# Two-layer hybrid trunk: rope tables kept on chip, deeper staging, inverses stored from two queues, waits of the side chains set anew

## The chip, the core and the metric

The kernel runs on one core of one Trainium2 chip. The metric is the device time of one execution in microseconds (us). TensorE is called PE, VectorE DVE, ScalarE ACT, GpSimd POOL, SyncE SP. SP issues nearly all DMAs; ACT issues a few. Each engine takes its instructions in the order of its own list, so an instruction that waits holds up all that stand behind it.

## The reference, cut to what matters

The model is two layers over 1024 tokens of width 1024 and 256 context tokens. Each layer projects the input by one wide matrix, runs three branches, merges them and normalizes.

```python
def _layer(...):                                  # twice
    u = x * (1 + scale) + shift                   # from silu(c) @ w_ada
    P, Pc = split_cols(u @ w_in), split_cols(uc @ w_in)
    q, k = axial_rope(P['a_q']), axial_rope(P['a_k'])
    y_a = band_ctx_attention(q, k, v, kc, vc, sink) * silu(P['a_z'])     # 8 heads, band of 128 and context
    y_b = layer_norm(depthwise_conv31(a * sigmoid(b))) ... * silu(P['b_z'])
    for d in range(2):                            # gated delta rule forwards and backwards
        T = triangular_solve(eye + A, eye)        # unit lower triangular, per chunk and head
        u, w = T @ (v * beta), T @ (k * beta * exp(gc))
        # scan over chunks: v_new = u - w @ S;  o = q_dec @ S + aqk @ v_new;  S = S * c_dec + k_dec^T @ v_new
    y_c = rmsnorm(o_forward + o_backward) * silu(P['c_z'])
    out = sum(sigmoid(gate_r) * (y_r @ w_branch[r]) for r in range(3)) @ w_out
    x = layer_norm(ALPHA * x + gate * out) * ln_g + ln_b
```

All arithmetic is float32. Dense products are made on PE as three products of a high and a low part (hi*hi, lo*hi, hi*lo).

## The kernel before

Channels lie on partitions, tokens on the free axis, in chunks of 256 (context), 512 and 512 tokens. A layer is a queue of dense pieces and a number of side chains, and PE's list is written by a planner while the program is built. The dense pieces (`main`) are projections of 128 output channels each: gates, gains, `aq`, `glu`, then the merge with `w_branch` and `finish` with `w_out`. The side chains are the recurrent delta branch (`delta1`, the inversion `invert`, `d2prep`, two `d2scan`), the attention units, the conformer and the norms. Each chain is a generator. After a step it yields a number of nanoseconds, and the planner puts at least that much estimated PE work, from `main` or from other chains, between this step and the chain's next one. These numbers stand in the table `W`, one for each layer:

```python
        if self.active and (self.active[0][0] <= self.pe or blocked or not self.main):
            c = self.active[0]
            self.pe = max(self.pe, c[0])
            ...
                w = next(c[2])
                c[0] = self.pe + (w or 0.0)
```

So PE's list is fixed, and on the chip PE waits whenever what a step needs comes later than the work put ahead of it. The order on DVE, ACT and SP is set by a scheduler when the program is built.

The places that the change touches:

- `load_half` (L236) loads half of a weight piece (`wraw`), ACT rounds it to `whi` (L244), DVE makes `wlo` (L247). Four buffers each.
- `rope` (L525) turns q and k. It loads 512 columns of the cosine and sine tables each time into `rtab`, of which there is one buffer; `conformer` uses the same buffer for `xt`.
- The tag `th` has three buffers of 128x512. They hold what goes out to or comes in from DRAM: `gth`, `fth`, `bth`, `r0`, `vr`, `vs`, `ar`, and in the merge `gt`.
- `invert` (L779) inverts the 32x32 diagonal blocks of both directions in 31 steps on DVE (`iU`), copies their transpose on ACT (`iV`, L819), and stores both to `sUB` by eight DMAs, all issued by ACT (L823).
- `d2prep` (L843) loads ten chunks of these blocks (`uc`), spreads them over block-diagonal tiles on DVE (`ud`, `ut`, `uh`), and joins them to full inverses by four rounds of products, with copies to `z`, `ut` and `ud` on ACT and DVE between. Its waits are `prep0` to `prep5`. `d2scan` takes the inverses (`scan1` to `scan3`).
- `attention` (L1133) loads K and V of one of two groups of heads into staging tiles of the tag `ks` (two buffers), makes K1, K2 and VH of them, and spawns one `att_unit` per 128 queries, two at a time. A unit loads `qs` (tag `ks` again), makes Q, waits `atq`, does its score products (`sd<-K,Q`, `ats` between heads), the softmax on DVE and ACT, waits `atm`, and transposes the weights and multiplies by V (`atp` between key blocks).
- `merge` (L1317) loads the branch results `y`, splits them (`yh`, `yl`), and multiplies by `w_branch`; it allocates the sums `acc` first.

DMAs from whatever engine take one of eight semaphores in turn (DMAHW0 to DMAHW7), and a DMA is issued only when the one that used its semaphore before has landed.

Of the kernel before, what the change touches and what calls it, by code (L numbers as in the profile page):

```python
# [8 lines left out]
F32 = mybir.dt.float32  # L9
# [3 lines left out]
ALU = mybir.AluOpType  # L13
# [4 lines left out]
P = 128  # L18
# [69 lines left out]
def constants():  # L88
# [6 lines left out]
    for d in range(2):  # L95
# [16 lines left out]
W = dict(rstd1=(510.0, 340.0), rstd2=(2820.0, 8120.0), adac=(6000.0, 11180.0), ss0=(15520.0, 10070.0),  # L112
         ss1=(560.0, 840.0), d1e=(3500.0, 3500.0), d1l=(2500.0, 2500.0), d1m=(1290.0, 880.0), d1t=(1120.0, 1270.0),
         prep0=(3500.0, 3500.0), do1=(17680.0, 17680.0), do2=(17680.0, 22350.0), atq=(3100.0,
         3540.0), ats=(2220.0, 1150.0), atm=(13300.0, 19000.0), atp=(1480.0, 1130.0),
         cf1=(38080.0, 38080.0), cf2=(5090.0, 12740.0), ln0=(2450.0, 4070.0), ln1=(1220.0,
         2790.0), ln2=(1120.0, 6710.0), d1s=(9710.0, 2570.0), dos=(9100.0, 20460.0),
         cfs=(139420.0, 35240.0), d2s=(20000.0, 20000.0), ada0=(35880.0, 35080.0),
         ln3=(9880.0, 13400.0), prep1=(2400.0, 2400.0), prep2=(2400.0,
         2400.0), prep3=(2200.0, 2200.0), prep4=(4500.0, 4500.0), prep5=(4000.0, 4000.0), scan1=(1540.0, 1540.0),  # L120
         scan2=(3090.0, 2630.0), scan3=(1380.0, 2190.0), ng=(9, 7), ln4=(1060.0, 1390.0),
         ln5=(1580.0, 130.0), g0=(3, 3), g1=(6, 6), g2=(16, 12), dvt=(13, 16), half=(0, 1),
         flight=(2, 2),
         inv0=(8000.0, 8000.0), inv1=(4000.0, 4000.0), inv2=(2300.0, 2300.0))


class Trunk:
# [4 lines left out]
    def __init__(self, ctx, tc, I, out, dbg=None):  # L132
        self.ctx, self.tc, self.nc, self.I, self.out = ctx, tc, tc.nc, I, out
        self.dbg = dbg or {}
        nc = self.nc
        ent = ctx.enter_context
        self.cst = ent(tc.tile_pool(name="cst", bufs=1))
        self.res = ent(tc.tile_pool(name="res", bufs=1))
        self.wp = ent(tc.tile_pool(name="wp", bufs=2))
        self.tp = ent(tc.tile_pool(name="tp", bufs=2))  # L140
        self.pp = ent(tc.tile_pool(name="pp", bufs=1, space=PSUM))
        self.dr = ent(tc.tile_pool(name="dr", bufs=1, space=DRAM))
        c = self.cst.tile([P, C_N], F32, name="consts")
        nc.sync.dma_start(c[:, :C_BAND], I["consts"][:, :C_BAND])
        self.late = lambda: nc.sync.dma_start(c[:, C_BAND:], I["consts"][:, C_BAND:])
# [223 lines left out]
    def first(self, S):  # L369
# [15 lines left out]
        with self.phase("ada0") as ph:  # L385
# [21 lines left out]
            self.late()  # L407
# [18 lines left out]
    def kv(self, l, S, ready):  # L426
# [4 lines left out]
        def back(c0, n, r):  # L431
            ps = self.sdps()
            for i in range(n // P):
                self.tr(ps[:, i * P:(i + 1) * P], r[:, i * P:(i + 1) * P])
            s = self.tp.tile([P, 512], F32, tag="th", name="vs", bufs=3)
            nc.scalar.activation(s[:, :n], ps[:, :n], AF.Copy)
            nc.sync.dma_start(S["V"][:, c0 // P:(c0 + n) // P, :], s[:, :n].rearrange("p (t c) -> p t c", c=P))

        def put(which, ps, c0, n):
            if which == 0:  # L440
                self.rope(ps, c0, n, lambda r, c0, n: nc.sync.dma_start(S["K"][:, c0:c0 + n], r))
                return
            r = self.tp.tile([P, 512], F32, tag="th", name="vr", bufs=3)
            nc.scalar.activation(r[:, :n], ps[:, :n], AF.Copy)
            pend.append((c0, n, r))
# [54 lines left out]
        for grp in ((CH_C, CH_A), (CH_B,)):  # L500
# [12 lines left out]
            for c0, n in grp:  # L513
# [8 lines left out]
                r = self.tp.tile([P, 512], F32, tag="th", name="ar", bufs=3)[:32]  # L522
# [258 lines left out]
    def invert(self, l, S, ph):  # L781
# [27 lines left out]
        for j in range(31):  # L809
# [283 lines left out]
    def glu(self, l, S, i, bg):  # L1093
# [15 lines left out]
    def gain(self, l, S, r, i):  # L1109
# [3 lines left out]
        def sink(ps, c0, n):  # L1113
            th = self.tp.tile([P, 512], F32, tag="th", name="fth", bufs=3)
# [17 lines left out]
    def attention(self, l, S, ph):  # L1132
# [8 lines left out]
        for g in range(2):  # L1141
            K1 = ph.tile([P, T], F32R, tag="K1", name="K1")
            K2 = ph.tile([P, T], F32R, tag="K2", name="K2")
            for c0, n in FULL:
                ks = ph.tile([P, 640], F32, tag="ks", name="ks", bufs=2)
# [5 lines left out]
            vs = ph.tile([P, NT, 64], F32, tag="ks", name="vs", bufs=2)  # L1151
# [4 lines left out]
            for t in range(0 if l < DEPTH - 1 else 2, NT):  # L1156
# [3 lines left out]
                self.spawn(name, self.att_unit(ph, S, g, t, K1, K2, VH, nsink[:, 4 * g:4 * g + 4], zero))  # L1160
# [3 lines left out]
    def att_unit(self, ph, S, g, t, K1, K2, VH, nsink, zero):  # L1164
# [7 lines left out]
        qs = ph.tile([P, 640], F32, tag="ks", name="qs", bufs=2)[:, :512].rearrange("p (h t) -> p h t", t=P)  # L1172
# [7 lines left out]
        yield self.w("atq")  # L1180
# [83 lines left out]
    def conformer(self, l, S, ph):  # L1264
# [14 lines left out]
        for t0 in range(0 if l < DEPTH - 1 else LCTX, T, N):  # L1279
# [286 lines left out]
```

## Time and profile before

| | |
|---|---|
| time, median of 3 runs | 2848.68 us (2844.78 to 2849.15) |
| the profiled execution | 2846.51 us |
| its span in the trace | 2844.5 us |
| PE busy | 2728.0 us, 96% of the span |
| DVE, ACT busy | 2236.0 us (79%), 1233.2 us (43%) |
| DMA | 481.04 MB, mean 169 GB/s |

The profile is of one execution. "PE" are the matmuls, whose ends are modelled and overlap slightly; PE idle in a stretch is its length less its busy time. "PEclk" is the share of the full 2.4 GHz that was granted; the clock has two levels, 1.2 and 2.4 GHz, so a mean of 0.85 tells that the lower level held for 30% of that stretch.

### The profile page before, as it was taken

The page shows a single profiled execution, that of the slowest core. Times are in us where ns is not written, and L with a number is a line of the kernel's source. Part 1 is how long each engine was busy: PE and PEld are TensorE (multiplying, and loading weights), DVE is VectorE, ACT ScalarE, POOL GpSimd, SP SyncE. Part 2 cuts the span into 40 slices and gives each one's busy share as a digit, 9 for nine tenths or more (in the row PEclk, how much of TensorE's full clock was granted, in tenths as well). Part 3 has the DMA queues.
Part 4 walks back from the last instruction along what each step waited for, and adds up shares of the span by engine and source line. Part 5 has one row for each costly group of instructions (what it writes and reads, how often), then busy time and mean ns, then how long its engine had stood idle before and what let it go on. Part 6 is the DMA issues. An engine that isn't in the chain of part 4 may idle for free.

```text
span 2844.5 us, 45774 instructions
## 1 busy us (share of the span) xinstructions
PE 2728.0 (96%) x15552; PEld 2316.8 (81%) x15552; DVE 2236.0 (79%) x5203; ACT 1233.2 (43%) x2718; POOL 18.4 (1%) x120
## 2 busy tenths in 40 slices
PE   7999999999999999999999999998899899997997
PEld 5888888888988888888877788787799788786877
DVE  5489979589957778768696588988998678775687
ACT  4454432223344555644354454532233455553344
POOL 0000000000000000000000000000000000000000
PEclk9999999999999999999999999999999999999999
DMA  8256564889534454367663354555786445535664
GB/s 302 90 188 186 162 199 143 225 233 259 160 101 126 122 159 126 114 205 230 192 197 126 106 153 146 172 146 164 204 233 197 137 124 150 157 96 168 197 216 152
DMA packets 537577, 481.04 MB, mean 169 GB/s; under 512 B 164832, under 2 KB 399872, under 8 KB 536576
## 3 DMA queue, kind: packets, MB, share of 16 engines
q1 hardware_dynamic: 536320, 472.88, 55.2%
q10 hardware_dynamic: 1024, 5.24, 0.7%
q8 instruction: 123, 2.02, 0.3%
q14 instruction: 110, 0.90, 0.1%
HBM read 338.42 MB, written 139.57 MB: 168 GB/s over the span
## 4 chain that ended last, share of the span: by engine, by line
PE 70%; DVE 15%; DMA 8%; ACT 3%; issue 2%; SPq 2%; ACTq 0%; DVEq 0%
PE mm L211 54%; PE sd L211 13%; DVE c L1261 4%; PE sd L216 3%; DVE wlo L247 1%; DMA E<-sGC 1%; DMA wada<-in_w_ada_dram 1%; DVE iU L816 1%; DVE iT L814 1%; DMA kt<-sKV 1%; DVE M L747 1%; DMA gt<-sG 1%; DVE ch L636 1%; DMA h<-sH 1%; DVE ch L635 1%
## 5 line engine op out<-in xcount | busy, mean ns | idle before, releaser
L211 PE MATMUL mm<-uhi,whi 128*128 128x512 f32 (+1 forms) x2936 | 1108.2, 377 | 14.0 <-ACT whi L244 11.7
L211 PE MATMUL mm<-uhi,wlo 128*128 128x512 f32 (+1 forms) x2936 | 1070.8, 365 | 3.1 <-DVE wlo L247 3.1
L211 PE MATMUL mm<-ulo,whi 128*128 128x512 f32 (+1 forms) x2936 | 1070.1, 364 | 2.1 <-DVE ulo L423 1.4
L211 PEld LDWEIGHTS mm<-uhi,whi 128*128 128x128 f32 x2936 | 558.9, 190 | 98.2 <-ACT whi L244 13.0
L211 PEld LDWEIGHTS mm<-uhi,wlo 128*128 128x128 f32 x2936 | 557.6, 190 | 94.0 <-DVE wlo L247 4.7
L211 PEld LDWEIGHTS mm<-ulo,whi 128*128 128x128 f32 x2936 | 559.2, 190 | 82.4 <-DVE ulo L423 4.1
L244 ACT ACTIVATE whi<-wraw 128x512 fp32r<-128x512 f32 x464 | 291.0, 630 | 570.8 <-PE mm L211 482.8
L1261 DVE SCALAR_TENSOR_TENSOR c<-h,hw,c 128x432 f32<-128x432 f32 (+3 forms) x720 | 425.4, 615 | 23.4 <-ACT c L1259 19.0
L247 DVE TENSOR_TENSOR wlo<-wraw,whi 128x512 fp32r<-128x512 f32 x464 | 316.4, 685 | 142.3 <-ACT whi L244 134.7
L211 PE MATMUL mm<-yh,whi 128*128 128x512 f32 (+1 forms) x480 | 182.2, 380 | 10.7 <-ACT yh L1328 10.0
L211 PE MATMUL mm<-yl,whi 128*128 128x512 f32 (+1 forms) x480 | 181.0, 377 | 3.2 <-DVE yl L1329 3.1
L211 PE MATMUL mm<-yh,wlo 128*128 128x512 f32 (+1 forms) x480 | 179.9, 375 | 1.5 <-DVE wlo L247 1.5
L1226 DVE TENSOR_TENSOR PTl<-sd,PTh 128x512 fp32r<-128x512 f32 x160 | 109.4, 688 | 55.5 <-ACT PTh L1225 33.8
L1225 ACT ACTIVATE PTh<-sd 128x512 fp32r<-128x512 f32 x160 | 94.5, 596 | 85.7 <-PE sd L211 43.1
L1126 ACT ACTIVATE gth<-mm 128x512 f32<-128x512 f32 (+1 forms) x120 | 65.4, 548 | 130.7 <-PE mm L211 93.9
L1203 ACT ACTIVATE Pt<-Pt,cl 128x640 f32<-128x640 f32 (+2 forms) x144 | 108.9, 759 | 19.4 <-DVE cl L1200 19.4
L211 PEld LDWEIGHTS mm<-yh,whi 128*128 128x128 f32 x480 | 91.4, 190 | 29.9 <-ACT yh L1328 11.0
L211 PE MATMUL sd<-K,Q 128*128 128x256 f32 (+1 forms) x544 | 96.8, 307 | 16.2 <-DVE Q L1178 11.9
L211 PEld LDWEIGHTS mm<-yl,whi 128*128 128x128 f32 x480 | 91.4, 190 | 23.5 <-DVE yl L1329 6.9
L211 PEld LDWEIGHTS mm<-yh,wlo 128*128 128x128 f32 x480 | 91.5, 191 | 18.6 <-DVE wlo L247 2.0
L211 PEld LDWEIGHTS sd<-K,Q 128*128 128x128 f32 x544 | 82.4, 190 | 28.5 <-DVE Q L1178 12.3
L216 PE MATMUL sd<-consts,Pt 128*128 128x128 f32 x640 | 96.3, 275 | 4.7 <-DVE Pt L1209 4.1
(282 smaller groups left out, 3547.0 us busy)
## 6 DMA issues: line engine op xcount, KB each, us to landing
wraw<-in_w_main_dram SPq DMA_DIRECT2D x248, 256.0 KB, 3.1
wraw<-in_w_branch_dram SPq DMA_DIRECT2D x120, 256.0 KB, 3.0
sG<-gth SPq DMA_DIRECT2D x96, 256.0 KB, 2.3
wraw<-in_w_out_dram SPq DMA_DIRECT2D x96, 256.0 KB, 3.1
gt<-sG SPq DMA_DIRECT2D x96, 256.0 KB, 3.0
aw<-in_w_ada_dram SPq DMA_DIRECT2D x32, 512.0 KB, 4.6
sME<-M SPq DMA_DIRECT2D x24, 640.0 KB, 5.4
sZ<-fth SPq DMA_DIRECT2D x48, 256.0 KB, 2.9
```

Of the source, the lines that this page charges most:

```text
L211: self.nc.tensor.matmul(out, lhsT, rhs, start=start, stop=stop)
L216: self.nc.tensor.transpose(out, x, self.ident[p0:p, p0:p])
L244: nc.scalar.activation(h, raw, AF.Copy)
L247: eng.tensor_tensor(q, raw, h.bitcast(F32), ALU.subtract)
L635: nc.vector.scalar_tensor_tensor(hh[:, a:b], pre[:, a + 1:b + 1], w(1), hh[:, a:b], ALU.mult, ALU.add)
L636: nc.vector.scalar_tensor_tensor(hh[:, a:b], pre[:, a + 2:b + 2], w(2), hh[:, a:b], ALU.mult, ALU.add)
L747: nc.vector.scalar_tensor_tensor(M[d][:, t - ta, 0:w, :], gv, C["betap"][:, t, c:c + 1], E[d][:, t - ta, :].unsqueeze(1).to_broadcast([P, ...
L1126: nc.scalar.activation(th[:, :n], ps[:, :n], AF.Tanh, scale=0.5)
L1203: nc.scalar.activation(Pt[j][:, :nk], Pt[j][:, :nk], AF.Exp, bias=negm[:, j:j + 1], scale=0.125, accum_out=den[:, j:j + 1])
L1225: nc.scalar.activation(hi, pt, AF.Copy)
L1226: nc.vector.tensor_tensor(lo, pt, hi.bitcast(F32), ALU.subtract)
L1261: nc.vector.scalar_tensor_tensor(c, h[:, a + j:b + j], hw[:, j:j + 1], c, ALU.mult, ALU.add)
```

## The change

The cosine and sine tables are loaded once, 1 MB, into a tile `tab` that stays; `rope` reads it and loads nothing. `th` gets five buffers instead of three, the attention staging `ks` four instead of two. `xt` gets a tile of its own. `invert` waits `inv3` before its copy and stores `iU` from SP and `iV` from ACT. The first two attention units of a group wait `at0` more before their scores. `merge` allocates `acc` after the first `y`. The table `W` has new numbers for 20 or so waits.

```diff
+        self.tab = self.cst.tile([P, 2, SEQ], F32, name="rope")
...
-            self.late()
+            nc.sync.dma_start(self.consts[:, C_BAND:], I["consts"][:, C_BAND:])
+            nc.sync.dma_start(self.tab, I["rope"])
...
-            tb = self.tp.tile([P, 2, 512], F32, tag="rtab", name="rtab", bufs=1)
-            nc.sync.dma_start(tb[:, :, :n], self.I["rope"][:, :, c0 - LCTX:c0 - LCTX + n])
+            tb = self.tab[:, :, c0 - LCTX:c0 - LCTX + n]
...
+        yield self.w("inv3")
         for p, sl in parts:
             nc.scalar.activation(V[p, sl], tr(U[p, sl]), AF.Copy)
         for X in (U, V):
             for d in range(2):
                 for dst, src in places(S["UB"][d if X is U else 1 - d, d], X, d):
-                    nc.scalar.dma_start(dst, src)
+                    (nc.sync if X is U else nc.scalar).dma_start(dst, src)
...
-                ks = ph.tile([P, 640], F32, tag="ks", name="ks", bufs=2)
+                ks = ph.tile([P, 640], F32, tag="ks", name="ks", bufs=4)
...
-                self.spawn(name, self.att_unit(ph, S, g, t, K1, K2, VH, nsink[:, 4 * g:4 * g + 4], zero))
+                self.spawn(name, self.att_unit(ph, S, g, t, K1, K2, VH, nsink[:, 4 * g:4 * g + 4], zero,
+                                               self.w("at0") if t < first + 2 else 0.0))
...
-        yield self.w("atq")
+        yield self.w("atq") + late
...
-        acc = ph.tile([P, KD, 512], F32, tag="xp", name="acc", bufs=2)
...
             ys = split(r)
+            if r == 2:
+                acc = ph.tile([P, KD, 512], F32, tag="xp", name="acc", bufs=2)
...
-                gt = self.tp.tile([P, 512], F32, tag="th", name="gt", bufs=3)
+                gt = self.tp.tile([P, 512], F32, tag="th", name="gt", bufs=5)
```

Of the table, the numbers that the prediction speaks of (first layer, second layer; the second is called layer 1 below, as in the code):

```diff
-atm=(13300.0, 19000.0), prep1=(2400.0, 2400.0), prep2=(2400.0, 2400.0), prep4=(4500.0, 4500.0)
+atm=(13300.0, 13000.0), prep1=(2900.0, 3200.0), prep2=(2900.0, 3000.0), prep4=(4500.0, 1500.0), at0=(1350.0, 9000.0)
```

How the change moves instructions, at three places of layer 1. First ACT's list where the inverses are stored (`iV` and `iU` are the transposed and the plain inverses, `r0` the copy that begins a rope, `whi` the rounded weights; in brackets the semaphores that the row waits for). Before:

```order
L530 ACTIVATE r0_20323<-mm_20294 128x512 [waits DMAHW0_49,PE_49]
L823 DMA sUB1_13061<-iU_19551 64x2048 [waits DMAHW2_49]
L823 DMA sUB1_13061<-iU_19551 32x1024 [waits DMAHW4_49]
L823 DMA sUB1_13061<-iU_19551 64x2048 [waits DMAHW6_49]
L823 DMA sUB1_13061<-iU_19551 32x1024 [waits DMAHW7_49]
L823 DMA sUB1_13061<-iV_19552 64x2048 [waits DMAHW0_49,Activation_49]
L823 DMA sUB1_13061<-iV_19552 32x1024 [waits DMAHW1_49,Activation_49]
L823 DMA sUB1_13061<-iV_19552 64x2048 [waits DMAHW4_49]
L823 DMA sUB1_13061<-iV_19552 32x1024 [waits DMAHW5_49]
L530 ACTIVATE r0_20384<-mm_20345 128x512 [waits PE_49]
L530 ACTIVATE r0_20419<-mm_20394 128x512 [waits DVE_49,PE_49]
L244 ACTIVATE whi_20436<-wraw_20435 128x512 [waits DMAHW3_49]
```

Now:

```order
L820 ACTIVATE iV_19508<-iU_19507 128x2048 [waits DVE_49,Pool_49]
L820 ACTIVATE iV_19508<-iU_19507 96x1024
L824 DMA sUB1_13031<-iV_19508 64x2048 [waits DMAHW4_49,Activation_49]
L531 ACTIVATE r0_20299<-mm_20272 128x512 [waits DMAHW0_49,PE_49]
L824 DMA sUB1_13031<-iV_19508 32x1024 [waits DMAHW0_49,Activation_49]
L824 DMA sUB1_13031<-iV_19508 64x2048 [waits DMAHW1_49]
L824 DMA sUB1_13031<-iV_19508 32x1024 [waits DMAHW4_49]
L531 ACTIVATE r0_20358<-mm_20319 128x512 [waits PE_49]
L244 ACTIVATE whi_20400<-wraw_20399 128x512 [waits DMAHW6_49]
L244 ACTIVATE whi_20406<-wraw_20405 128x512 [waits DMAHW7_49]
```

Four of the eight stores have left ACT's list; the last one that stays waits for DMAHW4, which the first one of them set. Both halves of one weight piece (`whi_20400`, `whi_20406`) now stand behind the stores, where one half (`whi_20436`) did.

Second, SP's list where layer 1's attention begins (`ks`, `vs`, `qs` stage K, V and Q; `o`, `o1` and `sZ` belong to other chains). Before:

```order
L1147 DMA ks_22803<-sK1_13055 64x512 [waits DMAHW1_49]
L1117 DMA sZ1_13064<-fth_22840 128x512 [waits DMAHW2_49,DVE_49]
L1060 DMA o_23049<-sO1_13062 128x512 [waits DMAHW3_49,Pool_49]
L1147 DMA ks_22808<-sK1_13055 64x512 [waits DMAHW6_49,DMAHW7_49,DMAHW4_49,DVE_49]
L1147 DMA ks_22808<-sK1_13055 64x512 [waits DMAHW5_49]
L1152 DMA vs_22814<-sV1_13054 128x10x64 [waits DMAHW1_49,DMAHW0_49,DVE_49]
L1061 DMA o1_23050<-sO1_13062 128x512
L1060 DMA o_23058<-sO1_13062 128x512
L1176 DMA qs_22819<-sQ1_13067 64x4x128 [waits DMAHW5_49,DMAHW4_49,DVE_49]
L1176 DMA qs_22819<-sQ1_13067 64x4x128 [waits DMAHW2_49]
```

Now:

```order
L1148 DMA ks_22677<-sK1_13025 64x512 [waits DMAHW0_49]
L1148 DMA ks_22682<-sK1_13025 64x512 [waits DMAHW1_49]
L1148 DMA ks_22682<-sK1_13025 64x512 [waits DMAHW2_49]
L1153 DMA vs_22688<-sV1_13024 128x10x64 [waits DMAHW3_49]
L1179 DMA qs_22693<-sQ1_13037 64x4x128 [waits DMAHW5_49,DMAHW6_49,DMAHW4_49,DVE_49]
L1179 DMA qs_22693<-sQ1_13037 64x4x128
L1179 DMA qs_22704<-sQ1_13037 64x4x128 [waits DMAHW7_49,DMAHW0_49,DVE_49]
L1179 DMA qs_22704<-sQ1_13037 64x4x128
```

The third `ks` and `vs` no longer wait for DVE to have done with an earlier buffer; only the two `qs` do. On PE the dense matmuls between the last product of the scan and the first score product are 30 before and 72 now.

Third, PE's list where layer 1's attention ends (`PTh`, `PTl` are the parts of the transposed softmax, `yh`, `yl` those of a branch result at the start of the merge). Before:

```order
L216 MATMUL sd<-consts,Pt 128x128 x4
L211 MATMUL sd<-PTh,VH 128x512
L211 MATMUL sd<-PTl,VH 128x512
L211 MATMUL sd<-PTh,VH 128x512
L211 MATMUL sd<-PTl,VH 128x512
L211 MATMUL mm<-yh,whi 128x512
L211 MATMUL mm<-yl,whi 128x512
```

Now:

```order
L211 MATMUL sd<-PTh,VH 128x512
L211 MATMUL sd<-PTl,VH 128x512
L211 MATMUL mm<-uhi,whi 128x512
L211 MATMUL mm<-ulo,whi 128x512
L211 MATMUL mm<-uhi,wlo 128x512
```

The merge's first product followed the last attention product directly; now 114 dense matmuls of the last gates stand between. Ahead of the last units' transposes 57 dense matmuls stand together now, and 18 did before.

## Rows read from the trace of the kernel before

**Rows 1.** Page, part 1: busy us, share of the span, instructions of each engine.

```profile
PE 2728.0 (96%) x15552; PEld 2316.8 (81%) x15552; DVE 2236.0 (79%) x5203; ACT 1233.2 (43%) x2718; POOL 18.4 (1%) x120
```

**Rows 2.** Busy time by stretch: length, then PE, PEld, DVE, ACT, POOL, PEclk, DMA share, GB/s.

```profile
500.00:725.00 225.00, 212.01 (x1559) 193.97 (x1558) 182.36 (x506) 68.42 (x193) 0.56 (x3) 0.98 0.86 237
1230.00:1290.00 60.00, 55.07 (x379) 51.42 (x377) 42.71 (x94) 27.89 (x54) 0.00 (x0) 0.91 0.77 241
1950.00:2060.00 110.00, 91.62 (x482) 76.39 (x481) 95.75 (x228) 30.93 (x58) 1.10 (x4) 0.94 0.77 210
2060.00:2205.00 145.00, 144.86 (x1038) 133.28 (x1037) 128.54 (x361) 49.71 (x135) 0.44 (x3) 1.00 0.78 215
2205.00:2240.00 35.00, 23.11 (x116) 19.83 (x115) 21.36 (x79) 12.55 (x34) 0.00 (x0) 0.85 0.58 173
2240.00:2562.00 322.00, 317.48 (x1613) 264.75 (x1612) 247.74 (x682) 173.59 (x394) 0.00 (x0) 1.00 0.43 129
2562.00:2600.00 38.00, 23.34 (x98) 16.96 (x97) 20.87 (x44) 18.23 (x38) 0.00 (x0) 0.82 0.40 121
```

**Rows 3.** Waits of PE in 1950 to 2060: us in total, times, longest.

```profile
PE mm L211 <- ACT whi L244: 10.5, 2, 7.2
PE sd L211 <- ACT z L879: 4.2, 3, 1.8
```

**Rows 4.** Timeline of ACT, 1948 to 1970: start, us, what [idle before <- releaser].

```profile
1950.35 4.13 ACT L819 ACTIVATE iV<-iU 128x2048 f32<-128x2048 f32 x1 [4.17 <-DVE iU L816]
...
1956.75 10.82 ACTq L823 DMA_DIRECT2D sUB<-iV  x4
1967.62 1.08 ACT L530 ACTIVATE r<-mm 128x512 f32<-128x512 f32 x2 [10.66 <-DMA sQ<-r]
```

**Rows 5.** Timeline of PE, 1961 to 1974.

```profile
1961.67 0.39 PE L211 MATMUL mm<-uhi,wlo 128*128 128x512 f32 x1
1969.27 0.79 PE L211 MATMUL mm<-uhi,whi 128*128 128x512 f32 x1 [7.21 <-ACT whi L244]
```

**Rows 6.** DMA issues: count, KB each, median us to landing.

```profile
rtab<-in_rope_dram SPq DMA_DIRECT2D x20, 512.0 KB, 4.5
...
sUB<-iV ACTq DMA_DIRECT2D x4, 512.0 KB, 6.8
```

**Rows 7.** Timeline of SP, 1940 to 2020.

```profile
1960.50 0.68 SPq L1091 DMA_DIRECT2D sQ<-r  x1
...
1998.47 0.56 SPq L243 DMA_DIRECT2D wraw<-in_w_main_dram  x1
```

**Rows 8.** Timeline of SP, 2205 to 2226.

```profile
2209.36 2.40 SPq L1147 DMA_DIRECT2D ks<-sK  x4
...
2213.30 1.09 SPq L1147 DMA_DIRECT2D ks<-sK  x2
...
2218.72 1.27 SPq L1176 DMA_DIRECT2D qs<-sQ  x2
...
2221.03 1.25 SPq L1176 DMA_DIRECT2D qs<-sQ  x2
```

**Rows 9.** Timeline of PE, 2206 to 2228.

```profile
2226.07 1.65 PE L211 MATMUL sd<-K,Q 128*128 128x256 f32 x5 [11.89 <-DVE Q L1178]
```

**Rows 10.** Timeline of PE, 2565 to 2592.

```profile
2570.39 1.88 PE L216 MATMUL sd<-consts,Pt 128*128 128x128 f32 x5 [4.10 <-DVE Pt L1209]
...
2591.41 0.79 PE L211 MATMUL mm<-yh,whi 128*128 128x512 f32 x1 [8.98 <-ACT yh L1328]
```

**Rows 11.** One unit's last score products (PE) and last softmax row (DVE).

```profile
2515.62 0.75 PE L211 MATMUL sd<-K,Q 128*128 128x256 f32 x4
...
2529.79 0.55 DVE L1209 TENSOR_SCALAR Pt<-Pt,cl 128x640 f32<-128x640 f32 x1
```

**Rows 12.** Waits in 500 to 725: one of PE, one of DVE.

```profile
PE sd L211 <- ACT z L879: 6.0, 4, 2.2
...
DVE kt L1003 <- DMA kt<-sKV: 13.5, 5, 4.4
```

More of the change, by code (lines that the diff above doesn't have):

```diff
@@ L108, in constants @@
     return c, np.ascontiguousarray(rope.astype(np.float32))
[L112 to L124, printed above, removed]
+W = dict(inv3=(2000.0, 2000.0), at0=(1350.0, 9000.0), rstd1=(510.0, 340.0), rstd2=(2820.0, 8120.0),
+         adac=(6000.0, 8180.0), ss0=(15520.0, 10070.0), ss1=(560.0, 840.0), d1e=(3500.0, 3040.0),
+         d1l=(2500.0, 2500.0), d1m=(1290.0, 880.0), d1t=(1120.0, 1270.0), prep0=(3500.0, 3500.0),
+         do1=(17680.0, 10610.0), do2=(17380.0, 22350.0), atq=(3100.0, 3540.0), ats=(2220.0, 1150.0),
+         atm=(13300.0, 13000.0), atp=(1110.0, 1130.0), cf1=(38080.0, 38080.0), cf2=(5090.0, 12740.0),
+         ln0=(2450.0, 2440.0), ln1=(1220.0, 2790.0), ln2=(1120.0, 6710.0), d1s=(9710.0, 2570.0),
+         dos=(9400.0, 20460.0), cfs=(139420.0, 35240.0), d2s=(20000.0, 20000.0), ada0=(35880.0, 35080.0),
+         ln3=(9880.0, 13400.0), prep1=(2900.0, 3200.0), prep2=(2900.0, 3000.0), prep3=(2200.0, 2200.0),
+         prep4=(4500.0, 1500.0), prep5=(7000.0, 3240.0), scan1=(1540.0, 2080.0), scan2=(3090.0, 3950.0),
+         scan3=(1380.0, 2190.0), ng=(9, 7), ln4=(1060.0, 1390.0), ln5=(1580.0, 130.0), g0=(3, 3), g1=(6, 6),
+         g2=(16, 12), dvt=(13, 16), half=(0, 1), flight=(2, 2), inv0=(8000.0, 8000.0), inv1=(4000.0, 4000.0),
+         inv2=(2000.0, 2300.0))
 class Trunk:
@@ L442, in put @@
                 return
-            r = self.tp.tile([P, 512], F32, tag="th", name="vr", bufs=3)
+            r = self.tp.tile([P, 512], F32, tag="th", name="vr", bufs=5)
             nc.scalar.activation(r[:, :n], ps[:, :n], AF.Copy)
@@ L521, in kv @@
                     yield
-                r = self.tp.tile([P, 512], F32, tag="th", name="ar", bufs=3)[:32]
+                r = self.tp.tile([P, 512], F32, tag="th", name="ar", bufs=5)[:32]
                 nc.scalar.activation(r[:, :n], ps[:32, :n], AF.Copy)
@@ L528, in rope @@
         nc = self.nc
-        r0 = self.tp.tile([P, 512], F32, tag="th", name="r0", bufs=3)
+        r0 = self.tp.tile([P, 512], F32, tag="th", name="r0", bufs=5)
         nc.scalar.activation(r0[:, :n], ps[:, :n], AF.Copy)
@@ L1113, in sink @@
         def sink(ps, c0, n):
-            th = self.tp.tile([P, 512], F32, tag="th", name="fth", bufs=3)
+            th = self.tp.tile([P, 512], F32, tag="th", name="fth", bufs=5)
             nc.scalar.activation(th[:, :n], ps[:, :n], AF.Tanh, scale=0.5)
@@ L1124, in sink @@
         def sink(ps, c0, n):
-            th = self.tp.tile([P, 512], F32, tag="th", name="gth", bufs=3)
+            th = self.tp.tile([P, 512], F32, tag="th", name="gth", bufs=5)
             nc.scalar.activation(th[:, :n], ps[:, :n], AF.Tanh, scale=0.5)
@@ L1150, in attention @@
             VH = ph.tile([P, NT, P], F32R, tag="VH", name="VH")
-            vs = ph.tile([P, NT, 64], F32, tag="ks", name="vs", bufs=2)
+            vs = ph.tile([P, NT, 64], F32, tag="ks", name="vs", bufs=4)
             nc.sync.dma_start(vs, S["V"][:, :, 64 * g:64 * g + 64])
@@ L1155, in attention @@
                                            ALU.mult, ALU.subtract)
-            for t in range(0 if l < DEPTH - 1 else 2, NT):
+            first = 0 if l < DEPTH - 1 else 2
+            for t in range(first, NT):
                 name = f"at{l}_{g}_{t}"
@@ L1300, in conformer @@
             rs = ph.tile([P, N], F32, tag="rs", name="rs")
-            xt = self.tp.tile([P, 2, 512], F32, tag="rtab", name="xt", bufs=1)
-            nc.vector.tensor_scalar(xt[:, 0, :N], ps, 2.0, LN_EPS, ALU.mult, ALU.add)
-            self.rsqrt(rs, xt[:, 0, :N], xt[:, 1, :N])
+            xt = ph.tile([P, 2, N], F32, name="xt")
+            nc.vector.tensor_scalar(xt[:, 0], ps, 2.0, LN_EPS, ALU.mult, ALU.add)
+            self.rsqrt(rs, xt[:, 0], xt[:, 1])
             nc.vector.tensor_tensor(c, c, rs.unsqueeze(1).to_broadcast([P, 4, N]), ALU.mult)
```

14 lines of the change are left out of this document (7 added, 7 removed).

## The prediction

> **What bounds the kernel now.** The first part of the page comes first: PE is busy for 2728.0 of the span's 2844.5 us [rows 1], so PE's list, fixed when the program is built, is the bound, and 116.5 us in which it stands idle are what there is to win, with whatever those pauses cost in clock. DVE at 79% is the only other engine near. The change leaves PE's work as it is, so a gain can only come out of PE's pauses. The second view, busy time by stretch, tells where they lie [rows 2]. PE idles 18.4 us in 1950 to 2060 (110 less 91.62), 11.9 in 2205 to 2240, 14.7 in 2562 to 2600, 13.0 in 500 to 725, 4.9 in 1230 to 1290: 62.9 of the 116.5 in five places that the change touches. The reader should also see the granted clock beside them: 0.94, 0.85, 0.82, 0.98 and 0.91, where a stretch without pauses has 1.00.
>
> To size what the clock adds I count half of the missing clock as loss: a pause is already counted as idle, and an idle PE loses nothing by a low clock, while the matmuls behind it do. The length times the missing share, halved, gives 3.3, 2.6, 3.4, 2.3 and 2.7 us. The five places then hold 21.7 (A), 14.5 (B), 18.1 (C), 15.3 (D) and 7.6 us (E), 77 together. The question is how much of each goes, and what new pauses come.
>
> **A: the stores of the inverses and the start of the second delta pass.** PE waits 10.5 us here for rounded weights in two pieces, the longest 7.2, and 4.2 us for `z` [rows 3]. The long one is ACT's doing: its last four stores hold its queue for 10.82 us from 1956.75, and the `r0` behind them begins at 1967.62 after 10.66 us of idleness that ended with the landing of `sQ`, a store of another queue [rows 4]. PE goes on at 1969.27 [rows 5]. That `sQ` store was issued at 1960.50 [rows 7]: the last `V` store used the semaphore that this one had set. In the new list the last `V` store waits for the first one's semaphore instead. The first is issued at 1956.75, as far as the rows tell, and such a store lands in 6.8 us at the median [rows 6], so ACT is free at about 1963.6, 4.0 us sooner. Against that, PE comes to its `whi` 12 matmuls sooner by the new order, 2.5 us, and two halves have to be rounded instead of one, about 1 us: the 7.2 shrinks by a little over 3 after the pause's front has moved with it, as the rest of the queue moves too. A 128x512 matmul took 0.39 us at the lower clock [rows 5], so I take 0.21 at the upper, here and below. The second weight wait, 3.3 us (10.5 less 7.2), has a load issued only at 1998.47, behind rope-table loads and `sQ` stores on SP [rows 7]. The table's 20 loads of 512 KB are gone [rows 6], and the order has two more weight pieces ahead there: all of it goes. Of the three `z` waits, 1.8 at the longest [rows 3], the 500 and 800 ns more in `prep1` (2.4 to 2.9 in layer 0, 3.2 in layer 1) and 500 and 600 in `prep2` take a third to a half each: 2 to 3.5 us. Sum 3 + 3.3 + 3 = 9.3, and 2.7 of the clock's 3.3: 12 us. Bounds 5 (ACT's queue no faster) to 19 (all but the stores' own latency).
>
> **B: the start of layer 1's attention.** PE stalls 11.89 us for the first `Q`, up to 2226.07 [rows 9]; so it ran out at 2214.18, and 30 matmuls (6.3 us) ahead of that the scan ended, near 2207.9. On SP the second `ks` is issued at 2213.30, 4 us behind the first, and `qs` at 2218.72 [rows 8]: with two buffers each load waits until an earlier one is used up. With four only `qs` waits, for the first `ks` copies, which frees it some 5.5 us sooner: `Q` is ready near 2220.6. 72 matmuls now cover 15.1 us, to 2223.0. The wait of 11.89 goes with 2.4 us to spare; with the clock 13 of 14.5 us. Bounds 9 (`qs` no sooner at all: 2226.07 less 2223.0 leaves a pause of 3) to 14.5.
>
> **C: the end of that attention.** Two stalls make 13.1 of the 14.7 us: 4.10 for the last softmax and 8.98 for `yh` [rows 10]. The change puts 57 matmuls ahead of the last transposes for 18, which is 8.2 us more, and 114 (24 us) between the last product and `yh` for none. Both stalls go, and nearly all of the clock's 3.4: 16 us, bounds 11 to 18.
>
> These matmuls are not new; they come out of the attention before, by `atm` of 13000 for 19000, and that is **F**. A unit's softmax ended 14.0 us after its last score products ended (2515.62 plus 0.75 to 2529.79 plus 0.55) [rows 11]. By the new order PE has some 15.7 us of work in between, where it had 21.5. That covers the unit shown by 1.7 us and none that is slower. Some of the 16 units will miss: I put 5 us, one in three by 1 us, bounds 0 to 14 (nearly every unit by 0.9). The `prep4` cut from 4500 to 1500 in layer 1 takes 3 us of cover from each of ten blocks. It is priced at nothing: the order leaves some 3 us there between the DVE copy and the product that reads it, which hides the copy; without that cover each block would lose up to 3.
>
> **D: layer 0's delta pass.** PE waits 6.0 us in four for `z`, and DVE 13.5 in five for `kt`, a load, the longest 4.4 [rows 12]; DMA is at 0.86 [rows 2], the highest of these stretches. `prep1` and `prep2` take 0.5 us from each `z` wait, two more `th` buffers let loads start earlier, but the transfers stay the same (10 of 481 MB leave, the rope table), and a DMA queue at 0.86 gives little for an earlier issue. 5 us, between 2 worse (loads issued earlier push `kt` back) and 12 better (all but 3 of the 15.3).
>
> **E: layer 0's first merge.** `gt` in five buffers and the later `acc` remove waits that I can't see singly: 2 us of 7.6, bounds 0 and 6.
>
> The rest costs nothing to the end: the table's load at the start, 1 MB, takes 4 us at this kernel's 237 GB/s [rows 2], most of it beside the first projections, which need no rope. The stores from SP stand ahead of loads there, four issues of about 0.7 us [rows 7], hidden by the weights already loaded.
>
> **The sum.** 12 + 13 + 16 + 5 + 2 less 5 is 43 us. The profiled execution took 2846.51 us, 2.0 over its span and 2.2 under the median of three: 2846.5 less 43 is 2803.5, and 2803 is my forecast.
>
> **A rule of the skill on A.** The Trainium skill, "DMA: Bandwidth & Descriptors", section "Issuing engines are not separate DMA queues", says that DMAs issued by different engines run on the same 16 DMA engines and interleave, so that a second issuer only saves issue time. By that rule the stores would land no sooner and A would give only its 3.3 and the `z` waits. The trace before shows a queue held for a semaphore, not for bandwidth: 10.66 us of idleness that one `sQ` landing ended, beside a DMA share of 0.77. So I take the row, and give the rule's outcome a chance of its own.
>
> **Rivals.** *The stores land no sooner.* DMA moves the same bytes; eight stores now begin within a few us of each other from two queues, and each takes longer than 6.8. Then the 7.2 stays, and grows by the 2.5 that PE comes earlier: A falls from 12 to about 6, total 37, 2809 us. For it: DMA is at 0.77 there. Against: the row of ACT's idleness.
>
> *DVE becomes the bound in layer 1.* Its busy times from 1950 to 2600 add to 514 of 650 us [rows 2], 79%; 43 us shorter makes it 84%, near the 81% at which 500 to 725 loses 5.8% of its time to PE's pauses. If the dense stretch from 2060 on (some 200 us of DVE-heavy blocks) then loses like that, 12 us come back, and D's 5 are not had either: 26 us gained, 2820. Against: 2060 to 2205 ran at DVE 89% with PE idle for 0.14 us.
>
> *Nothing measurable*: both of these and C's matmuls missed elsewhere, within 5.7 us of 2848.7.
>
> *Slower*: `atm`. If a unit's softmax takes 15.7 plus 3.0 us or more at the mean, because the units now overlap more dense work and DVE's other chains stand in front, 16 units give back 48 us, all that the rest gains (48 before F): above 18.7 us it is slower. At 20 us it is 16 times 4.3, 69 lost: 2868. For it: a stall here stops PE for all chains. Against: the unit in [rows 11] took 14.0, and DVE is at 248 of 322 us in that stretch [rows 2].
>
> **How the numbers follow.** The forecast, 2788 to 2820 as its own range (the terms' middle bounds), has 0.57 and the store rival, inside that range, 0.11; DVE 0.19; nothing measurable 0.06; slower 0.07. A measurement of this kernel can tell about 0.2%, 5.7 us, from no change (the three runs lie 4.4 apart). Faster is then 0.57 + 0.11 + 0.19 = 0.87. The range goes from 2782 (all terms near their better bounds: 18 + 14 + 17 + 11 + 4) to 2832, where DVE's case costs twice its 12: it leaves out some 2 in 10.
>
> **What will show it.** In the trace after: ACT's idleness behind the stores 5 to 7 us and not 10.66, and one weight wait of PE, not two (A); no wait for the first `Q` (B); no `yh` wait and PE busy to within 1 us through the last transposes (C); waits for `Pt` in layer 1 of 1 us here and there, 5 in all (F); the `z` waits in layer 0 near 4 us (D). The forecast is wrong if waits for `Pt` or `ut` in layer 1 pass 15 us, if the stall at the first `Q` stays, or if PE's idle sum isn't near 80 us.

## The result

The changed kernel takes 2782.22 us at the median of four runs (2779.09 to 2785.8); the kernel before, beside it, 2846.73. The ratio is 0.978 with an interval of 0.976 to 0.980: faster by 2.2%, 64.5 us, where 43 of 2846.5 were forecast (2803, range 2782 to 2832). The time lies at the very edge of the range, 0.2 us inside it. The profiled execution took 2785.8 us, its span is 2783.7, 60.8 below that of before.

Part 1 of the changed kernel's page, busy time by engine:

```profile
PE 2713.9 (97%) x15552; PEld 2308.2 (83%) x15552; DVE 2233.9 (80%) x5203; ACT 1229.4 (44%) x2718; POOL 18.6 (1%) x120
```

PE's idle time fell from 116.5 us to 69.8 (span less busy), 46.7 of the 60.8. The other 14.1 are in its busy time, which fell by as much at the same 15552 matmuls: fewer of them ran at the lower clock (the mean granted clock of the span was 0.986 and is 0.994). PE's idle sum, 69.8, is 10 us under the 80 that the prediction named as a sign. The stretches that answer to [rows 2], in the changed kernel's own time (length, then PE, PEld, DVE, ACT, POOL, PEclk, DMA share, GB/s):

```profile
500.00:725.00 225.00, 218.92 (x1634) 201.18 (x1633) 191.85 (x526) 67.32 (x184) 0.10 (x1) 0.99 0.80 218
1930.00:2040.00 110.00, 100.22 (x568) 85.61 (x567) 96.10 (x238) 33.80 (x65) 1.15 (x4) 0.98 0.74 194
2040.00:2180.00 140.00, 137.73 (x971) 125.14 (x970) 132.37 (x365) 48.29 (x132) 0.44 (x3) 1.00 0.78 213
2180.00:2215.00 35.00, 34.36 (x177) 28.95 (x176) 29.73 (x100) 18.93 (x54) 0.00 (x0) 1.00 0.72 219
2215.00:2500.00 285.00, 282.65 (x1455) 235.50 (x1454) 240.29 (x672) 166.19 (x382) 0.00 (x0) 1.00 0.43 128
2500.00:2545.00 45.00, 45.00 (x209) 37.05 (x208) 19.12 (x30) 17.04 (x29) 0.00 (x0) 1.00 0.62 199
```

The start of layer 1's attention (fourth row) idles 0.6 us for 11.9, its end (last row) nothing for 14.7, and both at the full clock, where before had 0.85 and 0.82. The inverses' stores (second row) still idle 9.8 us for 18.4. One stretch is worse: the rest of the second delta pass (third row) idles 2.3 us, where before had 0.14 in 2060 to 2205.

To give each stage its share, both traces were laid on one axis: PE's matmuls in their order, each counted with the mean distance from its start to the next one's for its kind. The difference of the two clocks at equal work, from one end of a stage to the other, is what the stage gained. Worked out from the rows of every matmul, in us against the trace of before; the runs e1 to e12 are the experiments below, and the last column adds a few stages without a pause:

```
                     start   D   att.0   E  1300-   A   pass    B    F     C    all
                                            1800
changed                3.2 10.6   0.0  1.1   2.7  11.0  -3.7  13.0  1.7  20.7  60.9
changed again (e12)    3.4 11.7   4.0  2.1   3.4  12.5  -2.8  13.0  1.4  20.7  70.7
e1 structure           3.2 11.2   2.3  1.7  -2.0   9.5   1.4   3.7  0.9  -1.0  31.0
e2 waits               1.2  6.8   0.8  2.3   4.7   5.0  -7.9   6.4  2.1  20.7  43.2
e3 atm 19000           1.4 10.5   3.3  0.6   4.4  12.7  -3.5  13.3 -0.1  -5.2  37.7
e4 prep4 4500          3.3 13.7   3.2  1.3   1.3  10.9  -0.5  12.9 -0.8   5.8  51.2
e5 rope loads          1.4  9.4   2.2  0.1   3.9   3.2  -4.6  13.0  2.0  20.7  51.4
e6 three th            2.9  9.6   2.2  0.3   1.5  11.8  -2.7  13.0  0.9  20.7  61.7
e7 stores from ACT     3.0  5.6   3.4  1.6   4.1   5.2  -4.4  13.0  1.9  20.7  55.1
e8 two ks              2.0 11.5   1.5  0.1   2.4  12.6  -1.4   3.5  1.8  20.7  55.5
e9 rope alone          0.4  6.4   2.5  2.9  -1.1   5.9  -3.1   0.2 -0.3  -0.2  14.0
e10 stores alone       0.8  7.2   0.8  1.6  -0.8   4.3   0.0  -2.1  0.5  -1.4  11.9
e11 prep4 2300         3.3  8.9   0.9  0.0   1.2  13.4  -6.8  13.0 -4.0  20.8  51.8
```

A to F are the prediction's terms, "att.0" is layer 0's attention, "pass" the second delta pass behind the stores. Each row is one execution. The first two rows are the same kernel: a sharp stall repeats to 0.1 us (B, C), while D, layer 0's attention and A differ by 1 to 4. Differences below 4 us in the soft columns say nothing. The traced execution of e11 was its slowest by 11 us.

What PE waits for in 1930 to 2040 of the changed kernel (us in total, times, longest), to be set beside [rows 3]:

```profile
PE sd L211 <- ACT z L880: 3.5, 3, 2.4
PE mm L211 <- ACT whi L244: 2.3, 1, 2.3
PE mm L211 <- DVE wlo L247: 2.3, 1, 2.3
```

The kernel before has, in its 1950 to 2060, a wait that the prediction didn't count:

```profile
PE mm L211 <- DVE wlo L247: 2.5, 2, 2.3
```

ACT behind the stores there, to be set beside [rows 4]:

```profile
1936.42 0.46 ACTq L824 DMA_DIRECT2D sUB<-iV  x1
...
1938.45 4.45 ACTq L824 DMA_DIRECT2D sUB<-iV  x3
1943.00 0.60 ACT L531 ACTIVATE r<-mm 128x512 f32<-128x512 f32 x1 [4.09 <-DMA sUB<-iV]
```

ACT now idles 4.09 us for the landing of its own first store (issued at 1936.42, queue free at 1943.0, 6.6 us later), where it idled 10.66 for an `sQ` store. One weight piece is waited for, not two. The `z` waits are hardly shorter here (3.5 us for 4.2).

Layer 1's attention from the first `Q` to 2500, all of PE's waits:

```profile
PE sd L211 <- DVE PTl L1229: 1.4, 3, 0.8
PE sd L211 <- DVE Q L1181: 0.6, 1, 0.6
PE sd L211 <- DVE cl L1193: 0.5, 2, 0.3
PE sd L216 <- DVE PTl L1229: 0.3, 1, 0.3
```

There is no wait for `Pt` at all, which is what F was to cost, and none for `yh` behind it.

### The profile page after: what moved, and what is told of

It reads as the page before. It is cut to its first block, busy times and chain, and to the rows that moved or that the text cites. A ratio compares the mean times of both kernels' runs of the same rounds, so it can differ in the third digit from the quotient of the medians.

```text
span 2783.7 us, 45676 instructions
## 1 busy us (share of the span) xinstructions
PE 2713.9 (97%) x15552; PEld 2308.2 (83%) x15552; DVE 2233.9 (80%) x5203; ACT 1229.4 (44%) x2718; POOL 18.6 (1%) x120
## 4 chain that ended last, share of the span: by engine, by line
PE 47%; DVE 11%; DMA 5%; ACT 2%; issue 2%; SPq 0%; ACTq 0%; DVEq 0%
PE mm L211 38%; PE sd L211 6%; DVE c L1264 3%; PE sd L216 2%; DVE wlo L247 1%; DMA kt<-sKV 1%; DVE iT L814 1%; DVE iU L816 1%; DMA uc<-sUB 0%; DMA sME<-M 0%; DVE PTl L1229 0%; DMA zt<-sZ 0%; DVE M L747 0%; DMA cv<-sCV 0%; DMA wraw<-in_w_main_dram 0%
## 5 line engine op out<-in xcount | busy, mean ns | idle before, releaser
L216 PEld LDWEIGHTS sd<-consts,Pt 128*128 128x128 f32 x640 | 77.9, 140 | 18.3 <-DVE PTl L1229 2.1
```

Of the source, the lines that this page charges most:

```text
L216: self.nc.tensor.transpose(out, x, self.ident[p0:p, p0:p])
```

## The experiments

Ratios are to the kernel before in runs on the same chip; the changed kernel stands at 0.978 (0.976 to 0.980), and in the last set at 0.976 (0.975 to 0.978).

**The two halves of the change.** e1 keeps all edits but the table:

```diff
-W = dict(inv3=(2000.0, 2000.0), at0=(1350.0, 9000.0), ... new table)
+W = dict(inv3=(0.0, 0.0), at0=(0.0, 0.0), ... table of before)
```

> All edits of the change but the table of waits, which is that of the kernel before (the two new waits are zero): PE's list is the one of before, row for row. Theory (the stores, the loads and the buffers give their part without any new pace): the start 3 us, the second weight wait and a sooner end of ACT's stores 6, the first Q 5.5 us sooner 6, layer 0's delta pass half of the 10.5 us that it gained, 5, nothing at the end of the attention; 20 us in sum, about 2826 us. Rival (the waits do it all, since PE's list decides): under 8 us, 2839 or more.

2815.47 us, ratio 0.990 (0.987 to 0.992): 31 us, half as much again as expected. The table of stages says where: D gave 11.2, all that the full change gave there, with PE's list as it was. A gave 9.5, B 3.7, C nothing. Its waits in A and at the first `Q`:

```profile
PE mm L212 <- DVE wlo L248: 6.2, 1, 6.2
...
PE sd L212 <- DVE Q L1182: 7.2, 1, 7.2
```

e2 is the other half, the kernel before with the new table and the two new waits:

```diff
-W = dict(... table of before)
+W = dict(inv3=(2000.0, 2000.0), at0=(1350.0, 9000.0), ... new table)
+        yield self.w("inv3")
-        yield self.w("atq")
+        yield self.w("atq") + late
```

> The kernel before with the new table and its two new waits alone: tables of rope loaded each time, three th and two ks buffers, all stores from ACT; PE's list is the one of the changed kernel. Theory: the end of the attention gives its 20 us in full, the first Q still comes 18 us after the scan and meets 16.3 us of cover, so 11 of its 13.9; the stores 1 of 11.4, since PE comes to its weights sooner and ACT is no sooner free; layer 0's delta pass 5; second delta pass 5 lost, the rest 4: 36 us, about 2811. Rival (the new paces need the sooner loads, and PE runs into them): under 22 us, 2825 or more.

2808.53 us, ratio 0.987 (0.985 to 0.989), 38 us and near the theory's 2811. C gave its 20.7 in full, so it belongs to the waits alone. At the stores and at the first `Q`:

```profile
PE mm L210 <- ACT whi L243: 9.9, 2, 7.5
...
PE sd L210 <- DVE Q L1180: 5.6, 1, 5.6
```

The 7.5 is the 7.2 of [rows 3], untouched by any pace. B needs both halves: without the buffers the 72 matmuls leave 5.6 us, without the matmuls the buffers leave 7.2. The halves add up to 69 us for 64; D above all is what they both claim (11.2 and 6.8, for 10.6 together).

**The end of the attention.** e3 and e4 each put one number of layer 1 back:

```diff
-atm=(13300.0, 13000.0)
+atm=(13300.0, 19000.0)
```

> The changed kernel with atm of layer 1 back at 19000. In PE's list the 114 matmuls between the last attention product and the first yh are gone (0 again), and 81 stand ahead of the last transposes. Theory (those 114 hide the split of y, and nothing else in this edit matters): the yh wait of 9 us and its clock come back, 12 us, and the waits for Pt stay away: about 2794 us. Rival (yh is sooner now for its own sake, by more th buffers and the later acc): within 4 us of the changed kernel, 2778 to 2786.

2809.18 us, ratio 0.987 (0.984 to 0.989): 27 us over the changed kernel, where the theory had 12. Both stalls are back, not `yh` alone:

```profile
PE mm L211 <- ACT yh L1329: 10.2, 2, 10.0
PE sd L216 <- DVE Pt L1212: 4.4, 1, 4.4
```

The 81 matmuls of the expectation stand one pair of units too early to help: in the trace they lie ahead of the transposes of the last pair but one (2479.0 to 2497.2), and between the last score products and the last transposes there is no dense matmul at all, where the changed kernel has 57 and the kernel before 18. With `atm` at 19000 the dense pieces run out before the end, so this edit takes both covers away, and the last softmax is waited for again:

```profile
2523.38 0.63 PE L211 MATMUL sd<-K,Q 128*128 128x256 f32 x4
2528.38 2.72 PE L216 MATMUL sd<-consts,Pt 128*128 128x128 f32 x8 [4.36 <-DVE Pt L1212]
```

Column C goes from +20.7 to -5.2.

```diff
-prep4=(4500.0, 1500.0)
+prep4=(4500.0, 4500.0)
```

> The changed kernel with prep4 of layer 1 back at 4500. In PE's list each of ten blocks has some 3 us more of dense work, and so none of it is left for the end of the attention (0 matmuls between the last product and the first yh, 51 ahead of the last transposes). Theory (the 4.8 us that the second delta pass lost are prep4's, and the cut is what pays for the cover at the end): 5 gained in the pass, 12 lost at the end, about 2789 us, with yh waits of 9 us and no z waits past 0.3 us in the pass. Rival (the loss in the pass has another cause, DVE's order in the denser blocks): z waits of 0.5 us stay, and about 2794 us.

2797.15 us, ratio 0.983 (0.981 to 0.985). Both parts of the theory hold in direction: C falls by 14.9 and the pass gains 3.2. The time is 8 us above the theory's 2789, nearer the rival's 2794, for the end costs more than the 12 that it was given. PE's waits at the end, and in the pass (2040 to 2180):

```profile
PE mm L211 <- ACT yh L1329: 10.6, 2, 10.2
...
PE sd L211 <- ACT ut L880: 1.3, 3, 0.6
```

The five `z` waits of the changed kernel in the pass (2.0 us, longest 0.5) are gone. The dense work that `prep4` gave up is the work that covers the split of `y` some 400 us later. The cut buys 15 us; what it costs in the pass, some 3, is no more than a soft column wavers by (e9, with the old `prep4`, loses 3.1 there too).

**The structural edits one by one**, each undone in the changed kernel; PE's list is the changed one in all four.

```diff
-            tb = self.tab[:, :, c0 - LCTX:c0 - LCTX + n]
+            tb = self.tp.tile([P, 2, 512], F32, tag="rtab", name="rtab", bufs=1)[:, :, :n]
+            nc.sync.dma_start(tb, self.I["rope"][:, :, c0 - LCTX:c0 - LCTX + n])
```

> The changed kernel with the rope table loaded again for each use, 20 loads of 512 KB into one buffer, as before; all else as changed. Theory (these loads and the single buffer are what held layer 0's delta pass and the second weight wait): 5 of the 10.5 us there come back and 4 at the inverses' stores, about 2791 us. Rival (the table's 10 MB of 480 are too little to matter, and the th buffers or the stores' queue are what helped): within 3 us of the changed kernel's 2782.

2796.79 us, ratio 0.985 (0.983 to 0.987). Loading the table again costs 8 us at the stores, twice what was put there, but 1 in D, where 5 were, although the DMA share in 500 to 725 is back at 0.86, at 237 GB/s. The traces are 9.9 us apart and the medians 14.6, since the changed kernel's trace is of its slowest execution. PE's waits in 1935 to 1995:

```profile
PE mm L210 <- ACT whi L243: 6.7, 2, 5.0
PE mm L210 <- DVE wlo L246: 3.8, 1, 3.8
```

```diff
-tag="th", ..., bufs=5
+tag="th", ..., bufs=3
```

> The changed kernel with three th buffers instead of five. Theory: the start loses 2 us again (PE's wait for vr at 50 us of before, a tile of th), layer 0's delta pass 3, the first merge 1: about 2788 us. Rival (no wait of any engine hung on these buffers): within 2 us of 2782, and no wait for vr.

2780.09 us, ratio 0.979 (0.977 to 0.981): the rival, and no wait for `vr`. The two more `th` buffers did nothing that shows.

```diff
-                    (nc.sync if X is U else nc.scalar).dma_start(dst, src)
+                    nc.scalar.dma_start(dst, src)
```

> The changed kernel with all eight stores of the inverses issued by ACT again. Theory (the eighth store waits for a semaphore whose transfer is late, and the weights' rounding behind it waits with it): ACT idles 9 us or more behind the stores for 4.1, PE's first weight wait grows by 4 to 6 us, layer 0 loses 1 to 2: about 2788 us. Rival (all DMAs share 16 DMA engines, so a second issuer lands nothing sooner): within 2 us of 2782 and ACT idle for 4 us as now.

2791.61 us, ratio 0.983 (0.981 to 0.985). The time is near the theory's, its mechanism isn't: with all the other edits in place ACT goes on at 1941.96, a microsecond sooner than in the changed kernel. What PE waits for is DVE (e7's timeline of DVE):

```profile
1942.04 6.09 DVE L1264 SCALAR_TENSOR_TENSOR c<-h,hw,c 128x342 f32<-128x342 f32 x10
...
1950.01 0.69 DVE L247 TENSOR_TENSOR wlo<-wraw,whi 128x512 fp32r<-128x512 f32 x1
```

The same place in the changed kernel:

```profile
1942.34 3.63 DVE L1264 SCALAR_TENSOR_TENSOR c<-h,hw,c 128x342 f32<-128x342 f32 x6
...
1946.51 0.68 DVE L247 TENSOR_TENSOR wlo<-wraw,whi 128x512 fp32r<-128x512 f32 x1
```

The scheduler that builds DVE's list put ten steps of the convolution ahead of `wlo` instead of six, 2.5 us, and two multiplications of a rope besides; PE's wait for `wlo` is 6.0 us for 2.3. An edit of one queue moved the list of another engine. D falls as well, from 10.6 to 5.6: the split of the stores in layer 0 is the one edit whose undoing costs that pass more than the 4 us of doubt.

```diff
-name="ks", bufs=4      (also "vs", "qs")
+name="ks", bufs=2
```

> The changed kernel with two staging buffers for K, V and Q instead of four. Theory (five us of the first Q are two round trips that the buffers enforce): the first Q product waits 5 to 7 us, with its clock 8 us lost in layer 1 and 1 or 2 elsewhere: about 2791 us. Rival (the 72 matmuls alone cover it): wait under 2 us, 2784 or less.

2789.2 us, ratio 0.982 (0.980 to 0.984), the theory, with a wait somewhat longer than its 5 to 7 us: PE's first score product.

```profile
2187.10 1.12 PE L211 MATMUL sd<-K,Q 128*128 128x256 f32 x3 [7.54 <-DVE Q L1181]
```

**Two structural edits alone, in the kernel before.** e9 has the table on chip (the edit of e5 the other way round, in the old kernel), e10 the split stores (that of e7).

> The kernel before with the rope table kept on chip and nothing else (all eight stores from ACT, three th and two ks buffers, old table of waits). Theory (without the 20 loads the eight semaphores are taken in another turn, so the last store no longer waits for an sQ store, and the second weight load is issued sooner): ACT's idleness behind the stores falls from 10.7 to under 6 us, the inverses' stretch of layer 1 gains 8 us, the start 2, all in all 10 to 13, about 2835. Rival (the wait is for transfers of the stores themselves, and stays while ACT issues all eight): ACT idles 9 us or more, and only the second weight wait and the start go, 5 us, about 2842.

2831.42 us, ratio 0.995 (0.993 to 0.997): the theory's size, the rival's mechanism. ACT still idles for an `sQ` store:

```profile
1947.31 7.96 ACTq L824 DMA_DIRECT2D sUB<-iV  x3
1955.31 1.08 ACT L532 ACTIVATE r<-mm 128x512 f32<-128x512 f32 x2 [8.78 <-DMA sQ<-r]
```

The stores' stretch gains 5.9, not 8; the theory's total was met by 6.4 us in D, which it hadn't put there.

> The kernel before with the plain inverses stored from SP and nothing else. Theory (two queues get the stores out sooner, and layer 0's first loads of the inverses with them): layer 0's delta pass gains 5, layer 1's stores 4 to 6, about 2837. Rival (with the rope loads still there the last store still waits for somebody else's semaphore, and SP's loads stand behind the stores): under 4 us, 2843 or more.

2835.63 us, ratio 0.997 (0.996 to 0.998): as the theory has it, and here ACT's queue is what the split frees:

```profile
1946.56 2.45 ACTq L823 DMA_DIRECT2D sUB<-iV  x3
1949.11 0.60 ACT L530 ACTIVATE r<-mm 128x512 f32<-128x512 f32 x1 [2.10 <-PE mm L211]
```

And yet A gains only 4.3, within the theory's 4 to 6 but half of what ACT's idleness lost, for PE's wait changed its name (1945 to 2015):

```profile
PE mm L211 <- DVE wlo L247: 8.0, 2, 7.2
PE mm L211 <- ACT whi L244: 2.8, 1, 2.8
```

**A middle value.** e11 gives the pass 0.8 us a block back and keeps 75 matmuls at the end; e12 is the changed kernel beside it.

```diff
-prep4=(4500.0, 1500.0)
+prep4=(4500.0, 2300.0)
```

> The changed kernel with prep4 of layer 1 at 2300 instead of 1500. In PE's list 75 matmuls (17 us) stand ahead of the first yh for 114 (26 us), and 8 us more lie in the second delta pass. Theory (the pass loses its 4 us to z waits that 0.8 us more a block would hide, and 17 us are enough for a yh wait of 10): 2 to 3 us faster than the changed kernel beside it. Rival (the gain at the end of the attention needs all 114, or the z waits don't care): equal or slower.

> The changed kernel once more, as it is, for comparison on the same chip as the three above: 0.978 of the kernel before, 61 to 64 us faster; any other result is the spread of such a comparison.

e11 took 2783.28 us, ratio 0.979 (0.977 to 0.982), e12 2776.8 us, 0.976 (0.975 to 0.978). 75 matmuls cover the end as well as 114 (20.8 and 20.7), but nothing was gained: 6.5 us slower than e12. The -6.8 of the pass comes from e11's slowest execution (2795.27, where the other three took 2782 to 2784). No version here beats the changed kernel. The later `acc`, `inv3`, `xt` and `at0` were not undone one by one, so what each is worth is not shown.

## Why the prediction was right, and where its sizes were off

A to D gained where the prediction put the gain. That the range still holds 64.5 us, by 0.2, is in part luck: the repetition e12, at 2776.8, lies outside it. What the 43 lacks is above all F's loss, which never came (6.7 us), and what D (5.6) and C (4.7) gave beyond their terms.

**A, 12 us: measured 11.0 and 12.5.** The chain was read rightly: ACT's queue, held by a semaphore that an `sQ` store had taken. e10 shows it alone (idleness 2.10 for 10.66), and the second weight wait went with the rope loads (e5 has one of 1.7 us back). That the total fits is partly luck: the waits for weights fell by 8.4 us (13.0 with the 2.5 for `wlo`, to 4.6) where 6.3 were put, the `z` waits by 0.7 where 3 were put; in e12 by 7.5 (to 5.5) and 3.4 (to 0.8). Two things were not seen. Behind ACT's wait stood DVE's convolution, which becomes the wait for `wlo` as soon as ACT is free (6.0 to 7.2 us at the longest in e1, e7 and e10). And e7 shows that with the other edits in place the split is no longer what frees ACT. The rival on the stores is refuted in its time. The gain was in ACT's queue behind the issue. The Trainium skill ("DMA: Bandwidth & Descriptors", "Issuing engines are not separate DMA queues") says that DMAs of several issuing engines run on the same 16 DMA engines and interleave, so that a second issuer only saves the time of issuing. The landings of the four large stores from ACT can't decide it: at the median they took 6.8 us before [rows 6], 6.6 in the changed kernel, but 5.4 with the split alone (e10) and 5.9 with it undone (e7).

**B, 13: measured 13.0.** e8, e1 and e2 show that neither buffers nor cover alone would have done it. The 2.4 us to spare were not there: the first score products begin 17.2 us behind the scan in the changed kernel and 14.3 in e1, where 12.7 were estimated, so the cover ended 0.6 us short.

**C, 16 with an upper bound of 18: measured 20.7.** The place and the 114 matmuls were right, as e3 and e4 show. The halving of the missing clock stands; the idle time was the term that was sized too small. Of the 13.7 us at the lower level that 0.18 of 38 us mean, 6.7 fell in the long pause, where they cost nothing, and the rest on matmuls (kernel before; the columns are those of [rows 2]):

```profile
2582.42:2591.41 8.99, 0.01 (x2) 0.01 (x1) 1.44 (x4) 1.22 (x2) 0.00 (x0) 0.63 0.43 125
2591.41:2600.00 8.59, 7.82 (x24) 5.49 (x25) 4.70 (x7) 3.15 (x5) 0.00 (x0) 0.79 0.74 229
```

The two stalls were put at 13.1 us. Counted from start to start, as in the table of stages, all pauses of the place cost 16.2: a stall in the rows begins at the modelled end of the matmul ahead, 0.39 long where the next could start after 0.23, and there are four more pauses of 0.2 to 0.5 us. The lower clock cost 3.7, for 3.4 put, and 0.4 is left over; this second count gives 20.3 for the table's 20.7. In B it finds 12.1 of pauses and 1.8 of clock, for 11.9 and 2.6 put.

**F, 5 lost: measured 1.7 gained,** the largest miss. The step took one unit's softmax of 14.0 us [rows 11] for typical. Worked out for all 16 units of layer 1 in both traces, from the end of a unit's last score product to its last `Pt` row, it was the slowest: the rest of before took 7.2 to 13.3, about half of them under 9. In the changed kernel they take 7.4 to 12.7 and have 15.1 to 16.4 us of cover. The estimate of the cover, 15.7, was right; the rival of late softmaxes died with it.

**D, 5: measured 10.6 and 11.7.** The step that failed is that a DMA share of 0.86 leaves little for an earlier issue. In 500 to 725 the rate fell from 237 to 218 GB/s, 4.3 MB or 8% of that stretch's traffic, and the share to 0.80; the share is 0.81 in e9 and 0.87 in e10, so the rope loads are what changed it. But the share does not go with the gain: e5 has 0.86 and gains 9.4, e7 has 0.81 and gains 5.6. The split of the stores, which the prediction gave nothing here, is what e7 lacks. Rope alone gives 6.4, the stores alone 7.2, the waits alone 6.8, and together 11: they all remove parts of the same pauses, and how they share them is not settled.

**E, 2: measured 1.1 and 2.1,** which a soft column can't tell from nothing.

**What was costed at nothing.** `prep4`: 3 to 4 us lost in the second pass in both traces of the changed kernel, and not hidden as the text had it: e4 takes the `z` waits away and gets 3.2 back, a size within the doubt of that column. The start: 3.2 us gained, between 0.4 and 3.4 over all kernels, and no edit orders them, so the cause stays open. 1300 to 1800: 1.2 to 4.7 us gained in all ten kernels with the new table, 0.8 to 2.0 lost in the three with the old one; each alone is within a soft column's doubt, and it was no term of mine. A smaller slip: the 0.39 us of [rows 5] is a matmul's length at the upper clock, not the lower, at which the products behind the pause before were 0.63 to 0.79 long. In the changed kernel's densest stretch they start 0.227 apart:

```profile
2525.63 0.39 PE L211 MATMUL mm<-ulo,whi 128*128 128x512 f32 x1
2525.86 0.39 PE L211 MATMUL mm<-uhi,wlo 128*128 128x512 f32 x1
```

The 0.21 used was near enough. **The sum** by stages: start 3.2, D 10.6, E 1.1, 1300 to 1800 2.7, A 11.0, the pass -3.7, B 13.0, F 1.7, C 20.7, and 0.6 between them: 60.9. The rival that DVE becomes the bound is not borne out beyond those 3.7: DVE is busy 132.37 of 140 us in the third stretch, 95%, and PE idles 2.3.

## What to carry to other kernels

Where PE's list is fixed, work is a stock: a microsecond of cover taken from a place that has slack (here `prep4` and `atm`) can be worth a whole stall at the end of a chain (15 us for `prep4`), and one must ask for each cut where that work will stand afterwards. Price a moved wait by the spread of all its instances, never by one row, and a removed transfer by the waits that end on it, not by its bytes, in the whole run or in one stretch: e5 brought 8% of a stretch's traffic back and cost 1 us there. When one engine's wait is taken away, read the next engine on the same chain before counting the whole of it as gained, and don't add edits that aim at the same pauses.

## What the runs showed of the hardware

DMAs of different queues are tied together by the turn of eight semaphores: ACT idled 10.66 us in one kernel and 8.78 in another for a store that SP had issued. Taking 20 loads away did not change that (the second of these kernels is e9); issuing four stores from SP did (e10, 2.10 us, and none of it for a DMA). At the same DMA share of 0.86 over 225 us, e5 gains 9.4 us there on the kernel before. And two profiles of one and the same kernel differed by 9.7 us in span (2783.7 and 2774.0), gathered in steps of up to 4 us over six stages, the largest in layer 0's attention, while the long stalls came out equal to 0.1 us.
